# Hybrid decoder layer: the gate branch's convolutions issued in steps, another order of two products, and later column sums

## The chip, the cores and the metric

The kernel runs on one core of one Trainium2 chip. The metric is device time in microseconds (us) of one launch; the two kernels are compared by their runs on the same chip. Engines: PE (TensorE, matrix products), DVE (VectorE), ACT (ScalarE), POOL (GpSimd) and SP (SyncE, which issues the DMAs). PE reads its operands from SBUF and writes to PSUM banks, which DVE and ACT empty.

## What is computed

One layer of a decoder for 1024 prompt tokens and 32 sample tokens (1056 columns in all): a token mixer with three recurrences, then a gated feed-forward part with a causal convolution of width 3 on its gate branch. The change touches the feed-forward part and the norms just before it:

```python
def rms_norm(x, w):
    xf = x.astype(jnp.float32)
    y = xf * lax.rsqrt(jnp.mean(xf * xf, axis=-1, keepdims=True) + EPS)
    return (y * w.astype(jnp.float32)).astype(x.dtype)

def conv_ffn(h, ffn_state, w_up, conv_w, conv_b, w_down):
    up = jnp.einsum('bld,df->blf', h, w_up)              # w_up: 1024 x 5632
    gate, val = up[..., :D_FF], up[..., D_FF:]           # D_FF = 2816
    gate, new_state = causal_dwconv(gate, ffn_state, conv_w, conv_b)
    out = jnp.einsum('blf,fd->bld', jax.nn.gelu(gate, approximate=True) * val, w_down)
    return out, new_state.astype(ffn_state.dtype)

# in run_trunk
x = x + rms_norm(mix, norm_mix_post[l])
hn = rms_norm(x, norm_ffn_pre[l])
f, nf = conv_ffn(hn, ffn_s[l], ...)
x = x + rms_norm(f, norm_ffn_post[l])
```

## The kernel before

Everything is kept with the features on the 128 partitions and the 1056 tokens as columns, in four quarters of 264 columns. Every float32 product is done as three products of rounded halves (high x high, high x low, low x high), so a weight tile is first split: a cast on ACT (`wh`) and a subtraction on POOL or DVE (`wl`, L272 or L1834).

**Who orders the work.** The kernel's Python text makes several streams (generators), and `Weave` (L121 and after) takes turns among them by rank and by a planner's clock, `weave.now`, that counts matmul columns at 2.4 GHz: 0.11 us for one matmul of 264 columns, and four times that for one in plain float32. A stream that yields a number of nanoseconds, such as `WAIT["f_rows"]`, is continued once the planner's clock has gone that far. The instructions so issued go to a scheduler, which orders each engine's queue by priority (the order of issue, or 400 instructions earlier under `tc.high_priority(offset=AHEAD)`) among those whose inputs its own model of time holds for ready. On the chip each engine then runs its queue strictly in that order.

**The norms, `finish(q)` (L1603 and after).** For each quarter q the output projection's 8 row blocks (`product`, 24 matmuls each) are squared and summed into `sqs[q]`. `finish(q)` loads a quarter of x (one buffer, `x`, for all quarters), sums over the partitions by a matmul with ones (`rstd_of`, PSUM tile `po`), scales and adds (L1616, L1617), squares again on ACT into `sx`, adds on DVE into `ss` (L1624), waits `WAIT["f_rows"]`, sums over the partitions once more (the second `po`, which reads `ss`) and makes the operands of the next stage (L1634, L1581). `finish(1)` starts when `finish(0)` has made its x.

**The up projection.** From row block 4 on, pairs of row blocks are done as a `fast` task: a scheme of seven products of half-size blocks in place of eight, numbered p = 1 to 7, each for two halves u = 0, 1 of the columns. One product `run(p, u)` is 12 matmuls of 264 columns. Gate tasks (gate rows i) and value tasks (value rows i-1) alternate; i goes from 2 to 10, with a value task at either end, 20 tasks in all. Products 1, 6, 5, 2, 7 belong to the current task, while 4 and 3 of the task before are done between them, so that the list in `up()` (L1938) is the order of PE's queue:

`(1,0) (1,1) (6,0) (4,0)' (4,1)' (6,1) (3,0)' (3,1)' (5,0) (5,1) (2,0) (2,1) (7,0) (7,1)`

with a prime for the previous task's. In each u, 1 and 2 share a bank of `accp` (2 buffers), 6, 7 and 4 one of `accr` (5 buffers), 5 and 3 another. The bank of product 2 is emptied by a value task at L1817 (`hid`), and product 1 of the next task wants that buffer; (6,1) wants the bank that (4,0)' leaves, which a value task empties at L1810 (`rs`). With a gate task's product (3,1)' its `end()` is called: it issues both row blocks' `gate_conv` (L1772): small copies on POOL, a scaling on ACT (L217, Identity), two scalar_tensor_tensor instructions of 1072 columns on DVE (L1782), and Gelu on ACT. Its result `fy` is read by the value task after the next gate task.

**The weight pieces.** A product's weights are cast (L1833) and split (L1834) once for both u. `weight_piece` takes half tiles from a ring: two pieces share a pair of tiles (`wh`, `wl`), there are two such pairs, and a pair can be written again when every product that reads either half is done. The order of the pieces is 1, 6, 4', 3', 5, 2, 7. Since seven is odd, the pairs of a value task are (1, 6), (4', 3'), (5, 2), (7 and the next task's 1), and those of a gate task (6, 4'), (3', 5), (2, 7). So in a value task the piece of 5 can be cast once (6,1) is through. Products 2 and 4 split on DVE, the others on POOL. The sums that make the pieces (L1867 to L1872) run ahead of their task.

Of the kernel before, what the change touches and what calls it, by code (L numbers as in the profile page):

```python
# [8 lines left out]
F32 = mybir.dt.float32  # L9
# [7 lines left out]
P = 128  # L17
# [51 lines left out]
WAIT = dict(  # L69
    inv4=3140, blocks_in=7470, blocks_out=12000, inv=1760, out=3400, rows=3000, exp=690, gdn_unit=3720,  # L70
    norms=2680, kk=3700, scan1=460, scan2=1130, scan3=480, norm=6000, ml_unit=1120, ml_decay=1780, ml_kq=1330,
    ml_kw=1020, ml_scan=1070, ml_post=3000, gate=5000, ssd_x=1540, ssd_b=1170, ssd_decay=4000, ssd_scan=1020,
    ssd_unit=6650, ssd_post=2800, s_decay=3970, state=430, s_hop=2530, outer=760, s_ml=3230, s_out=2100,
    s_norm=6310, rows1=9000, rows2=6960, rows3=8500, f_rows=12500, f_wait=7000, f_piece=2600,
)

WARM = 8
# [77 lines left out]
def drain(gen):  # L155

    while True:
        try:
            next(gen)
        except StopIteration as e:  # L160
            return e.value
# [28 lines left out]
def bc(ap, ax, n):  # L190
    a = ap.unsqueeze(ax)
    s = list(a.shape)
    s[ax] = n
    return a.to_broadcast(s)
# [3 lines left out]
def kernel(ctx: ExitStack, tc: tile.TileContext, I, O):  # L198
# [17 lines left out]
    def act(**kw):  # L216
        i = nc.scalar.activation(**kw)  # L217
        if kw["func"] in (AF.Exp, AF.Tanh, AF.Gelu_apprx_tanh):
            others.append(i)
        return i  # L220
# [31 lines left out]
    def col(v, p=P, p0=0):  # L252
        return vec[p0:p0 + p, v:v + 1]
# [56 lines left out]
    def rstd_of(r, ssum):  # L310

        ps = sump.tile([P, 512], F32, name="po")
        n = r.shape[-1]
        for s in ssum:
            mm(ps[:, :n], lhsT=ones, rhs=s, start=(s is ssum[0]), stop=(s is ssum[-1]))
        log = nc.scalar.activation(out=r, in_=ps[:, :n], func=AF.Ln, scale=1.0 / D, bias=epsc)
        in_order(log, tables[-1])
        nc.scalar.activation(out=r, in_=r, func=AF.Exp, scale=-0.5)
        return r
# [51 lines left out]
    with ExitStack() as ph:  # L371
# [563 lines left out]
        pre, early_gdn = {}, {}  # L935
# [639 lines left out]
        def split_quarter(q, i, by_tile=False):  # L1575

            hi, lo = ops[q][0][i], ops[q][1][i]
            for a, b in [(k, k + 1) for k in range(KH)] if by_tile else [(0, KH)]:
                x = mx[:, KH * i + a:KH * i + b, quarters[q]]
                nc.scalar.copy(out=hi[:, a:b], in_=x)  # L1580
                vtt(out=lo[:, a:b], in0=x, in1=hi[:, a:b].bitcast(F32), op=ALU.subtract)  # L1581

        def new_operand(q):
            t = [block(hnp.tile([P, T], F32R, name=f"h{(0, 4, 13, 8)[q] + i}")) for i in range(4)]
            ops[q] = t[:2], t[2:]
# [17 lines left out]
        def finish(q):  # L1603
            if q:
                yield lambda: ("x", q - 1) in have
            x = on.tile([P, KD, Q], F32, name="x")
            dma(out=x, in_=I["xQ"][q])
            yield WAIT["f_wait"]
            s = sqs[q]
            r = rstd_of(on.tile([P, Q], F32, name="rstd", bufs=2), [s[:, 0, :], s[:, 1, :]])  # L1610
            sx = on.tile([P, KH, Q], F32, name="sx")
            s = on.tile([P, 2, Q], F32, name="ss", bufs=4)
            for i in range(2):
                ks = slice(KH * i, KH * i + KH)
                m = mx[:, ks, quarters[q]]
                vtt(out=m, in0=m, in1=bc(r, 1, KH), op=ALU.mult)  # L1616
                vtt(out=x[:, ks], in0=x[:, ks], in1=m, op=ALU.add)  # L1617
                if i == 0:
                    act(out=sx, in_=x[:, ks], func=AF.Square)
                    vtt(out=sx[:, 0:2], in0=sx[:, 0:2], in1=sx[:, 2:4], op=ALU.add)  # L1620
                else:
                    for a in (KH, KH + 2):
                        act(out=sx[:, 2:4], in_=x[:, a:a + 2], func=AF.Square)
                        vtt(out=sx[:, 0:2] if a == KH else s, in0=sx[:, 0:2], in1=sx[:, 2:4], op=ALU.add)  # L1624
                dma(out=x1_dram[q, :, ks], in_=x[:, ks])
            for k in range(KD):
                act(out=mix[k][:, quarters[q]], in_=x[:, k, :], func=AF.Copy, scale=col(V_FPRE + k))
            have.add(("x", q))
            yield WAIT["f_rows"]
            r = rstd_of(on.tile([P, Q], F32, name="rstd", bufs=2), [s[:, 0, :], s[:, 1, :]])  # L1630
            new_operand(q)
            for i in range(2):
                m = mx[:, KH * i:KH * i + KH, quarters[q]]
                vtt(out=m, in0=m, in1=bc(r, 1, KH), op=ALU.mult)  # L1634
                split_quarter(q, i)
            have.add(("normed", q))
# [56 lines left out]
    with ExitStack() as ph:  # L1693
# [4 lines left out]
        fo = []  # L1698
# [47 lines left out]
        def samp6(t, a):  # L1746
            return t[:, a:a + 48].rearrange("p (b s) -> p b s", s=6)
# [21 lines left out]

        ffn_io = {}  # L1770

        def gate_conv(f, pre):  # L1772
            st_ffn, ffn_o = ffn_io["st"], ffn_io["out"]
            y = fo[0].tile([P, 1074], F32, name="fy", bufs=4)
            blk = samp6(pre, 1026)
            nc.gpsimd.memset(pre[:, 0:2], 0.0)
            gcopy(out=blk[:, :, 0:2], in_=st_ffn[:, f, :].rearrange("p (b s) -> p b s", s=2))
            gcopy(out=ffn_o[:, f, 0:2], in_=pre[:, 1024:1026])
            gcopy(out=ffn_o[:, f, 2:18].rearrange("p (b s) -> p b s", s=2), in_=blk[:, :, 4:6])
            act(out=y[:, :LF], in_=pre[:, 2:2 + LF], func=AF.Identity, bias=col(V_FB + f), scale=col(V_FW + 3 * f + 2))  # L1780
            for j in (1, 0):
                stt(out=y[:, :LF], in0=pre[:, j:j + LF], scalar=col(V_FW + 3 * f + j), in1=y[:, :LF],  # L1782
                    op0=ALU.mult, op1=ALU.add)
            act(out=y[:, :LF], in_=y[:, :LF], func=AF.Gelu_apprx_tanh)
            return y

        def new_pre():
            return fg.tile([P, 1080], F32, name="fpre", bufs=4)
# [1 line left out]
        def gate_task(i):  # L1790
            pres = [new_pre() for j in range(2)]

            def out(j, h, u, x, ps):
                gate_in(pres[j], 2 * u + h, x, ps)

            def end():
                ys[i] = [gate_conv(2 * i + j, pres[j]) for j in range(2)]
            return fast(i, 0, out, end)

        def value_task(i):  # L1800
# [111 lines left out]
        ys = {}  # L1912

        def up():
            yield lambda: "projected" in have
            pres = [new_pre() for f in range(PLAIN)]
            for q in range(NQ):
                yield lambda: ("normed", q) in have
                for f in range(PLAIN):
                    ps = yield from dense(accr, held["up", f], operand, KD, q, Q)  # L1920
                    gate_in(pres[f], q, None, ps)
                have.add(("plain", q))
            yield lambda: "pieces" in have
            places.update({1: new_n(8, F32), 6: new_n(9, F32), "raw": new_n(10, F32)})
            ffn_io["st"] = fo[0].tile([P, NF, 16], F32, name="st_ffn")
            ffn_io["out"] = fo[0].tile([P, NF, 18], F32, name="ffn_o")
            dma(out=ffn_io["st"], in_=I["st_ffn"])
            tasks = [(value_task, 0)]
            for i in range(PLAIN // 2, NF // 2):
                tasks += [(gate_task, i), (value_task, i - 1)]  # L1930
            tasks.append((value_task, NF // 2 - 1))
            prev = None
            for n, (task, i) in enumerate(tasks):
                cur = task(i)
                if n == 0:
                    for i in range(PLAIN // 2):
                        ys[i] = [gate_conv(2 * i + j, pres[2 * i + j]) for j in range(2)]
                for p, u in ((1, 0), (1, 1), (6, 0), (4, 0), (4, 1), (6, 1), (3, 0), (3, 1),  # L1938
                             (5, 0), (5, 1), (2, 0), (2, 1), (7, 0), (7, 1)):
                    if p in (4, 3):  # L1940
                        if prev:
                            yield from prev.run(p, u)
                            if (p, u) == (3, 1):
                                prev.end()
                    else:
                        yield from cur.run(p, u)
                prev = cur
            for p, u in ((4, 0), (4, 1), (3, 0), (3, 1)):
                yield from prev.run(p, u)
            prev.end()  # L1950
            dma(out=O["ffn"], in_=ffn_io["out"])
# [5 lines left out]
        fo = fo[0]  # L1957
# [196 lines left out]
```

## Time and profile before

| | us |
|---|---|
| median of the 3 runs shown | 1596.19 (1593.82 to 1618.47) |
| the profiled execution, its own time | 1594.29 |
| span of its profile | 1592.5 |
| mean granted TensorE clock | 0.973 of full |

Stages in the profile: the mixer until about 720 us, the end of the mixer and the output projection with its norms until about 812, four plain gate row blocks until about 860, the 20 `fast` tasks until about 1310, the down projection to the end. Times in the profile are from the start of the span. PE's row counts matmuls whose ends are modelled; the idle time in front of an instruction is in square brackets, with what released it.

### The profile page before, as it was taken

What the parts mean: (1) busy time and instruction counts of PE and PEld (TensorE: products, weight loads), DVE (VectorE), ACT (ScalarE), POOL (GpSimd) and SP (SyncE); (2) the same over time, 40 slices, a digit from 0 to 9 for tenths busy, and PEclk for the clock granted to TensorE, in tenths of its full rate; (3) what the DMA queues carried; (4) which work ended last, traced back from release to release, by engine and by line L of the source; (5) the groups of instructions that cost most, each with busy time, mean ns of one, the idle gap of its engine ahead of it and who ended that gap; (6) DMA issues with size and microseconds to landing.
All of it is one profiled execution on the core that took longest, in us unless ns stands there. A gap on an engine that the chain in (4) does not pass through costs nothing.

```text
span 1592.5 us, 27521 instructions
## 1 busy us (share of the span) xinstructions
PE 1461.3 (92%) x10756; PEld 1414.0 (89%) x10756; DVE 1014.6 (64%) x2019; ACT 622.1 (39%) x1348; POOL 587.2 (37%) x666
## 2 busy tenths in 40 slices
PE   9788998989999989896899999999999999999995
PEld 8788898979989989894899988889999899999995
DVE  6898878795484366626578566666565666234457
ACT  7653544433432332434566223333332234111244
POOL 6244333232444542564224323333333232212323
PEclk9999999999999999998899999999999999999998
DMA  6011111011121232224330212221212126312303
GB/s 218 29 49 29 32 37 34 25 30 30 56 61 40 69 112 83 81 93 148 135 121 32 81 68 81 74 73 42 81 68 81 68 94 232 126 45 96 118 28 137
DMA packets 59786, 124.92 MB, mean 78 GB/s; under 512 B 15480, under 2 KB 21496, under 8 KB 58632
## 3 DMA queue, kind: packets, MB, share of 16 engines
q1 hardware_dynamic: 59656, 123.16, 23.2%
q8 instruction: 85, 1.39, 0.4%
q14 instruction: 45, 0.37, 0.1%
HBM read 97.40 MB, written 25.21 MB: 77 GB/s over the span
## 4 chain that ended last, share of the span: by engine, by line
PE 52%; DVE 25%; ACT 8%; issue 6%; POOL 5%; DMA 3%; SPq 0%; DVEq 0%; ACTq 0%; POOLq 0%
PE acc L208 43%; DVE fy L1782 4%; PE mb L208 3%; PE mc L208 3%; DVE kq L471 2%; DMA E<-rows_dram 2%; PE mb L212 2%; POOL wl L1834 2%; ACT wh L1833 1%; PE po L208 1%; DVE ws L1867 1%; DVE two L790 1%; DVE v L471 1%; POOL E L874 1%; ACT fy L217 1%
## 5 line engine op out<-in xcount | busy, mean ns | idle before, releaser
L208 PE MATMUL acc<-h,wh 128*128 128x264 f32 (+1 forms) x3040 | 680.5, 314 | 38.9 <-DVE hid L1817 21.7
L208 PEld LDWEIGHTS acc<-h,wh 128*128 128x128 f32 x3040 | 498.8, 192 | 48.6 <-ACT fy L217 23.4
L208 PE MATMUL acc<-h,wl 128*128 128x264 f32 (+1 forms) x1528 | 467.4, 306 | 2.6 <-POOL wl L272 2.4
L208 PEld LDWEIGHTS acc<-h,wl 128*128 128x128 f32 x1528 | 291.8, 191 | 3.9 <-POOL wl L272 2.6
L208 PE MATMUL acc<-hidl,wh 128*128 128x264 f32 x576 | 163.7, 284 | 0.5 <-DVE hidl L1973 0.5
L208 PE MATMUL acc<-hidh,wh 128*128 128x264 f32 x576 | 163.9, 285 | 0.0
L208 PE MATMUL acc<-hidh,wl 128*128 128x264 f32 x576 | 163.5, 284 | 0.0
L1834 POOL TENSOR_TENSOR wl<-ws,wh 128x512 fp32r<-128x512 f32 x60 | 82.6, 1384 | 179.1 <-ACT wh L1833 179.1
L1996 DVE TENSOR_TENSOR fa<-fa,acc 128x264 f32<-128x264 f32 x160 | 68.0, 427 | 124.7 <-PE acc L208 123.9
L272 POOL TENSOR_TENSOR wl<-w,wh 128x1024 fp32r<-128x1024 f32 x42 | 102.9, 2451 | 51.6 <-ACT wh L271 48.1
L208 PE MATMUL acc<-n,wh 128*128 128x264 f32 x640 | 119.0, 284 | 1.2 <-DVE n L1902 1.2
L208 PEld LDWEIGHTS acc<-hidl,wh 128*128 128x128 f32 x576 | 108.6, 189 | 0.8 <-DVE hidl L1973 0.8
L1834 POOL TENSOR_TENSOR wl<-w,wh 128x512 fp32r<-128x512 f32 x40 | 62.9, 1574 | 124.4 <-ACT wh L1833 118.6
L208 PEld LDWEIGHTS acc<-hidh,wl 128*128 128x128 f32 x576 | 108.6, 189 | 0.0
L208 PEld LDWEIGHTS acc<-hidh,wh 128*128 128x128 f32 x576 | 108.5, 188 | 0.0
L1987 POOL TENSOR_TENSOR wl<-w,wh 128x1024 fp32r<-128x1024 f32 (+1 forms) x22 | 47.6, 2164 | 148.2 <-ACT wh L1986 145.2
L208 PE MATMUL acc<-r,wh 128*128 128x264 f32 x480 | 90.8, 286 | 11.7 <-DVE rs L1810 11.7
L208 PEld LDWEIGHTS acc<-n,wh 128*128 128x128 f32 x640 | 99.1, 189 | 1.4 <-issue 1.4
L208 PE MATMUL acc<-n,wl 128*128 128x264 f32 x320 | 90.8, 284 | 0.0
L208 PEld LDWEIGHTS acc<-r,wh 128*128 128x128 f32 x480 | 74.2, 188 | 13.5 <-DVE rs L1810 13.5
L1782 DVE SCALAR_TENSOR_TENSOR fy<-fpre,vec,fy 128x1072 f32<-128x1072 f32 x44 | 75.8, 1775 | 13.4 <-ACT fy L217 13.3
L1986 ACT CAST wh<-w 128x1024 fp32r<-128x1024 f32 (+1 forms) x22 | 20.5, 933 | 132.2 <-PE acc L208 127.5
(527 smaller groups left out, 3042.3 us busy)
## 6 DMA issues: line engine op xcount, KB each, us to landing
w<-in_w_in_dram SPq DMA_DIRECT2D x30, 512.0 KB
w<-in_w_up_dram SPq DMA_DIRECT2D x60, 256.0 KB
hid_dram<-hid SPq DMA_DIRECT2D x22, 528.0 KB
hidl<-hid_dram SPq DMA_DIRECT2D x21, 528.0 KB
w<-in_w_dn_dram SPq DMA_DIRECT2D x17, 512.0 KB
w<-in_w_out_dram SPq DMA_DIRECT2D x16, 512.0 KB
E<-rows_dram SPq DMA_DIRECT2D x24, 256.0 KB
n<-in_w_up_dram SPq DMA_DIRECT2D x20, 256.0 KB
```

The costliest lines, as they stand in the source:

```text
L208: return nc.tensor.matmul(out, **kw)
L212: return nc.tensor.transpose(out, in_, identity)
L217: i = nc.scalar.activation(**kw)
L272: tt(out=wl[:, ks], in0=w[:, ks], in1=wh[:, ks].bitcast(F32), op=ALU.subtract)
L471: stt(out=y[:, a:b], in0=pre[:, a + j:b + j], scalar=cw2[:, 4 * t + j:4 * t + j + 1], in1=y[:, a:b], op0=ALU.mult, op1=ALU.add)
L790: vtt(out=two[pr], in0=NT[pr, :, pr], in1=bc(con[pr, C_LOW:C_LOW + 2 * B16], 1, 4), op=ALU.mult)
L874: gtt(out=E, in0=E, in1=bc(con[:, mask:mask + P], 1, n), op=ALU.add)
L1782: stt(out=y[:, :LF], in0=pre[:, j:j + LF], scalar=col(V_FW + 3 * f + j), in1=y[:, :LF], op0=ALU.mult, op1=ALU.add)
L1834: tt(out=wl, in0=x, in1=wh.bitcast(F32), op=ALU.subtract)
L1986: nc.scalar.copy(out=wh, in_=w)
L1987: gtt(out=wl, in0=w, in1=wh.bitcast(F32), op=ALU.subtract)
L1996: vtt(out=fa[:, q, m, :], in0=fa[:, q, m, :], in1=ps[:, :Q], op=ALU.add)
```

## The change

Three edits. `gate_conv` becomes a generator with four steps (copies and Identity, each of the two scalar_tensor_tensor, Gelu), its result tile being made by `end()` through `new_y`. `end()` puts the two generators on a list, and `up()` takes one step of it after every product with u = 1, seven times a task. In the list of products (3,0)' and (6,1) change places. `WAIT["f_rows"]`, 12.5 us for every quarter, becomes 24, 15.5, 15.5 and 12.5 us. The number of instructions stays as it is.

```diff
--- before.py
+++ after.py
@@ -71,7 +71,7 @@
     norms=2680, kk=3700, scan1=460, scan2=1130, scan3=480, norm=6000, ml_unit=1120, ml_decay=1780, ml_kq=1330,
     ml_kw=1020, ml_scan=1070, ml_post=3000, gate=5000, ssd_x=1540, ssd_b=1170, ssd_decay=4000, ssd_scan=1020,
     ssd_unit=6650, ssd_post=2800, s_decay=3970, state=430, s_hop=2530, outer=760, s_ml=3230, s_out=2100,
-    s_norm=6310, rows1=9000, rows2=6960, rows3=8500, f_rows=12500, f_wait=7000, f_piece=2600,
+    s_norm=6310, rows1=9000, rows2=6960, rows3=8500, f_rows=(24000, 15500, 15500, 12500), f_wait=7000, f_piece=2600,
 )
 
 WARM = 8
@@ -1626,7 +1626,7 @@
             for k in range(KD):
                 act(out=mix[k][:, quarters[q]], in_=x[:, k, :], func=AF.Copy, scale=col(V_FPRE + k))
             have.add(("x", q))
-            yield WAIT["f_rows"]
+            yield WAIT["f_rows"][q]
             r = rstd_of(on.tile([P, Q], F32, name="rstd", bufs=2), [s[:, 0, :], s[:, 1, :]])
             new_operand(q)
             for i in range(2):
@@ -1769,20 +1769,35 @@
 
         ffn_io = {}
 
-        def gate_conv(f, pre):
+        def new_y():
+            return fo[0].tile([P, 1074], F32, name="fy", bufs=4)
+
+        def gate_conv(f, pre, y):
+
             st_ffn, ffn_o = ffn_io["st"], ffn_io["out"]
-            y = fo[0].tile([P, 1074], F32, name="fy", bufs=4)
             blk = samp6(pre, 1026)
             nc.gpsimd.memset(pre[:, 0:2], 0.0)
             gcopy(out=blk[:, :, 0:2], in_=st_ffn[:, f, :].rearrange("p (b s) -> p b s", s=2))
             gcopy(out=ffn_o[:, f, 0:2], in_=pre[:, 1024:1026])
             gcopy(out=ffn_o[:, f, 2:18].rearrange("p (b s) -> p b s", s=2), in_=blk[:, :, 4:6])
             act(out=y[:, :LF], in_=pre[:, 2:2 + LF], func=AF.Identity, bias=col(V_FB + f), scale=col(V_FW + 3 * f + 2))
+            yield
             for j in (1, 0):
                 stt(out=y[:, :LF], in0=pre[:, j:j + LF], scalar=col(V_FW + 3 * f + j), in1=y[:, :LF],
                     op0=ALU.mult, op1=ALU.add)
+                yield
             act(out=y[:, :LF], in_=y[:, :LF], func=AF.Gelu_apprx_tanh)
-            return y
+            yield
+
+
+        later = []
+
+        def one_later():
+            while later:
+                if next(later[0], 0) == 0:
+                    later.pop(0)
+                else:
+                    break
 
         def new_pre():
             return fg.tile([P, 1080], F32, name="fpre", bufs=4)
@@ -1794,7 +1809,8 @@
                 gate_in(pres[j], 2 * u + h, x, ps)
 
             def end():
-                ys[i] = [gate_conv(2 * i + j, pres[j]) for j in range(2)]
+                ys[i] = [new_y() for j in range(2)]
+                later.extend(gate_conv(2 * i + j, pres[j], ys[i][j]) for j in range(2))
             return fast(i, 0, out, end)
 
         def value_task(i):
@@ -1934,8 +1950,10 @@
                 cur = task(i)
                 if n == 0:
                     for i in range(PLAIN // 2):
-                        ys[i] = [gate_conv(2 * i + j, pres[2 * i + j]) for j in range(2)]
-                for p, u in ((1, 0), (1, 1), (6, 0), (4, 0), (4, 1), (6, 1), (3, 0), (3, 1),
+                        ys[i] = [new_y() for j in range(2)]
+                        for j in range(2):
+                            drain(gate_conv(2 * i + j, pres[2 * i + j], ys[i][j]))
+                for p, u in ((1, 0), (1, 1), (6, 0), (4, 0), (4, 1), (3, 0), (6, 1), (3, 1),
                              (5, 0), (5, 1), (2, 0), (2, 1), (7, 0), (7, 1)):
                     if p in (4, 3):
                         if prev:
@@ -1944,6 +1962,8 @@
                                 prev.end()
                     else:
                         yield from cur.run(p, u)
+                    if u:
+                        one_later()
                 prev = cur
             for p, u in ((4, 0), (4, 1), (3, 0), (3, 1)):
                 yield from prev.run(p, u)
```

## Rows read from the trace of the kernel before

**Rows 1.** The page's first two lines: the span and PE's share.
```profile
span 1592.5 us, 27521 instructions
PE 1461.3 (92%) x10756; PEld 1414.0 (89%) x10756; DVE 1014.6 (64%) x2019; ACT 622.1 (39%) x1348; POOL 587.2 (37%) x666
```

**Rows 2.** What PE waited for, whole span: total us, times, longest.
```profile
PE acc L208 <- DVE hid L1817: 21.7, 9, 2.4
PE po L208 <- DVE ss L1624: 17.1, 3, 12.2
PE acc L208 <- DVE rs L1810: 11.7, 9, 1.4
```

**Rows 3.** Chain of waits, 780 to 1310 us: start, us, what.
```profile
966.93 4.41 PE acc L208 x23
...
1013.31 3.06 PE acc L208 x23
...
1022.15 21.98 PE acc L208 x179
...
1284.66 22.16 PE acc L208 x168
```

**Rows 4.** Timeline around a value task's end, DVE and PE: start, us, instruction [idle before].
```profile
1004.47 7.15 DVE L1782 SCALAR_TENSOR_TENSOR fy<-fpre,vec,fy 128x1072 f32<-128x1072 f32 x4 [1.39 <-ACT fy L217]
...
1012.75 0.76 DVE L1817 TENSOR_TENSOR hid<-fy,acc 128x264 f32<-128x264 f32 x2
...
1013.31 0.48 PE L208 MATMUL acc<-h,wh 128*128 128x264 f32 x2 [2.41 <-DVE hid L1817]
```

**Rows 5.** Timeline early in a gate task, DVE and PE.
```profile
1018.46 1.75 DVE L1867 TENSOR_TENSOR ws<-w 128x512 f32<-128x512 f32 x1 [2.85 <-POOL wl L1834]
...
1021.08 0.68 DVE L1870 TENSOR_TENSOR w<-w 128x512 f32<-128x512 f32 x1
1021.68 0.41 DVE L1810 TENSOR_TENSOR rs<-n,acc 128x264 f32<-128x264 f32 x1
...
1022.15 0.51 PE L208 MATMUL acc<-r,wh 128*128 128x264 f32 x2 [1.32 <-DVE rs L1810]
```

**Rows 6.** Timeline in a value task, ACT, POOL, PE: the piece of 5.
```profile
999.06 0.41 PE L208 MATMUL acc<-h,wh 128*128 128x264 f32 x2
...
999.19 0.62 ACT L1833 CAST wh<-ws 128x512 fp32r<-128x512 f32 x1 [5.35 <-PE acc L208]
...
999.89 1.29 POOL L1834 TENSOR_TENSOR wl<-ws,wh 128x512 fp32r<-128x512 f32 x1 [6.58 <-ACT wh L1833]
...
1001.99 0.41 PE L208 MATMUL acc<-n,wh 128*128 128x264 f32 x2
```

**Rows 7.** Timeline, POOL and DVE: a piece beside L1782, L1782 alone, an early memset.
```profile
1004.58 2.37 POOL L1834 TENSOR_TENSOR wl<-w,wh 128x512 fp32r<-128x512 f32 x1
...
865.74 1.33 DVE L1782 SCALAR_TENSOR_TENSOR fy<-fpre,vec,fy 128x1072 f32<-128x1072 f32 x1
...
987.83 0.11 POOL L1776 MEMSET fpre<- 128x2 f32 x1
```

**Rows 8.** Timeline of the norms, PE, SP, ACT and DVE.
```profile
739.78 1.96 PE L208 MATMUL po<-ss,ones 128*128 128x264 f32 x4
...
759.55 2.13 PE L208 MATMUL po<-ss,ones 128*128 128x264 f32 x4 [12.17 <-DVE ss L1624]
...
810.56 1.16 PE L208 MATMUL po<-ss,ones 128*128 128x264 f32 x4 [1.65 <-DVE ss L1624]
...
757.17 1.72 ACT L217 ACTIVATE mix<-x,vec 128x264 f32<-128x264 f32 x4
...
759.34 0.37 SPq L1607 DMA_DIRECT2D x<-in_xQ_dram  x1
...
767.44 2.42 DVE L1617 TENSOR_TENSOR x<-x,mix 128x1056 f32<-128x1056 f32 x2
...
772.92 0.71 DVE L1624 TENSOR_TENSOR ss<-sx 128x528 f32<-128x528 f32 x1 [0.71 <-ACT sx L217]
```

## Prediction, as put on record before the run

> **What bounds the kernel now.** I read the page's shares first: PE is busy 92% of the span [rows 1], so whatever does not let PE run on earlier is worth nothing, and the most that can be won is PE's idle time and the time at a lower clock. PE's waits over the whole span came next [rows 2]: three of the groups there belong to the three edits, 21.7 us for `hid` (9 times), 11.7 us for `rs` (9 times) and 17.1 us for the second column sum (3 times), 50.5 us together. The reader is to see that the first two are small waits that come back once in each pair of tasks, and the third is mostly one wait of 12.17 us. Then the chain of waits over the `fast` tasks [rows 3], for what a matmul costs and what a wait does to the clock: 179 matmuls take 21.98 us, 0.1228 us each, so a product of 12 takes 1.47 us. The 23 matmuls behind a wait for `hid` take 3.06 us in one pair and 4.41 us in another. Last the timelines around one wait of each kind.
>
> **The wait for `hid`.** At 1004.47 DVE starts the four L1782 of a gate task's `end()` in one block, 7.15 us [rows 4]. Product (2,0) of the value task has begun meanwhile and is through at about 1006.4, but L1817, which empties its bank, stands behind the block and two weight sums and starts at 1012.75. PE has done (2,1) and (7,0), (7,1) by 1010.9 and stands for 2.41 us until (1,0) of the next task gets the bank. The change issues the four L1782 one to every second product, so that at most one is issued between two emptyings of banks. Three products lie between the end of (2,0) and (1,0), 3 x 1.47 = 4.4 us. One L1782 costs 1.33 us alone [rows 7] and 7.15 / 4 = 1.79 us in the block; even a block of two (3.6 us) ahead of L1817 (0.4 us) would be through in time. I take the wait as gone: -21.7 us, bounds 0 and -21.7. Where the stall goes: (4,0) wants the reads of (7,0), which have 1.47 us for each of the four products (7,1), (1,0), (1,1), (6,0), so nothing is late next there.
>
> **The clock.** The longer runs of matmuls stand behind waits for `hid`: 4.41 - 3.06 = 1.35 us, twice in the nine pairs, and at 1284.66 168 matmuls take 22.16 us where 168 x 0.1228 = 20.6, 1.5 us more [rows 3]. Without the 2.4 us waits in front I take these as gone too: -4.2 us, bounds 0 and -4.2.
>
> **The wait for `rs`.** In a gate task PE wants the bank that (4,0)' leaves for (6,1). L1810, which empties it, stands behind the sums made ahead for the next task, L1867 (1.75 us, begun only when POOL has freed its tile), L1868 and L1870 (0.68 each), and ends at 1021.68 + 0.41 = 1022.09; PE waits 1.32 us [rows 5]. (3,0)' now runs in that gap: it needs no new bank, and its piece, whose split is what L1867 waits for, is ready at 1018.46, while PE falls idle at 1022.15 - 1.32 = 1020.83. PE would want the bank 1.47 us later, at 1022.3. So -11.7 us, with a margin of only 0.1 to 0.2 us; bound on the other side below, with the rivals.
>
> **What the new order costs.** In a value task the piece of 5 can be cast once (6,1) is through. There (6,1) ended at 999.06, the cast began at 999.19 and POOL was done at 999.89 + 1.29 = 1001.18, 2.1 us behind (6,1); (5,0) began at 1001.99 behind two products, and nothing waited [rows 6]. With (3,0)' ahead of (6,1), one product is left between, 1.47 us, and the third matmul of (5,0), the first that reads `wl`, comes 0.25 us later. 2.1 - 1.72 = 0.4 us, in the 10 value tasks that have a task in front: +4.0 us. PE's whole queue stands behind that matmul; the banks have time to spare then. The lower bound is 0; the upper one stands with the rivals. The other pairs keep 2.3 us or more: that of 3' and 5 in a gate task has (6,0), (4,0)', (4,1)', 4.4 us, for the same 2.1, and that of 2 falls from 5.9 to 4.4 us.
>
> **The steps themselves** are the same instructions on the same engines. The Identity and the Gelu on ACT and the copies on POOL move by at most half a task, and their reader is more than a task away. I cost them at nothing; their cover is that ACT and POOL are busy 39% and 37% [rows 1]. No DMA is moved past another by any of the three edits.
>
> **The later sums.** `finish(1)` starts its first sum at 739.78 [rows 8]. It stands 7 us (`f_wait`) behind the place from which `finish(0)`'s `f_rows` counts. From there the planner now gives 15.5 us to `finish(1)`'s second sum and 24 - 7 = 17 us to `finish(0)`'s, in place of 12.5 and 5.5: the two change places. By the planner's 0.11 us a matmul, less 0.88 for the first sum itself, `finish(1)`'s second sum now stands behind 133 matmuls, where it stood behind 108. 42 of them are done when PE falls idle at 759.55 - 12.17 = 747.4, the other 91 take 11.2 us, so PE gets there at about 758.6. But its input is the L1624 that ended at 772.92 + 0.71 = 773.6, and this does not hang on PE: x has one buffer, which ACT left at 757.17 + 1.72 = 758.9, its load was issued at 759.34, and L1617 ran at 767.44. So the wait of 12.17 us goes from one sum to the other. What is won is the order on DVE: L1634 and L1581 of `finish(0)` no longer run ahead of L1617, which can start when the load lands. I estimate 1 to 2 us from that, and 31 matmuls more done by the second sum against a longer stretch at half clock come out within 1 us. I take -1.5 us; bounds +3 (three emptyings of banks, on ACT ahead of the copy that frees x) and -18 (both waits gone and PE not slowed). For quarter 2 the wait of 1.65 us [rows 8] has 3 us more: -1.7. Sum of this edit: -3.2.
>
> **Sum.** -21.7 - 4.2 - 11.7 + 4.0 - 3.2 = -36.8 us, on the profiled execution's own 1594.3 us (its span is 1592.5, 1.8 lie around it, and it is 1.9 us under the median of the runs shown): 1557.5, say 1558 us, 2.3% less. 2% is about what a measurement of this kernel can tell from no change; it lies at 1562.
>
> **Rivals.**
> - *The scheduler puts the steps back together.* The order of issue is not the order of a queue: POOL ran the memset of L1776 at 987.83, 14 us before the place where `end()` issues it [rows 7]. If DVE again gets four L1782 in a row, the waits for `hid` and the clock stay and 11.7 - 4.0 + 3.2 = 10.9 us are won: 1583. Against it: an emptying of a bank is now issued ahead of three of the four, so that the scheduler must prefer it once ready. Chance 0.12.
> - *`rs` still waits.* If one L1782 of the second row block, now issued in the gate task, starts ahead of L1810, the margin of 0.1 is gone and PE waits 1.2 to 1.7 us in 9 gate tasks: about 13 us, 1571. For it: DVE idles 2.85 us ahead of L1867, where such a step fits only if it starts early [rows 5]. Chance 0.15.
> - *A step meets the piece that PE waits for.* A POOL split takes 1.29 us alone [rows 6] and 2.37 beside L1782 [rows 7]. If a step ran beside the piece of 5, the new wait would be 0.4 + 1.1 = 1.5 us in 10 tasks: 11 us more, 1569. For it: four steps are spread over two tasks now; against it, by issue the steps end with (3,1) of the gate task, before any value task's (6,1). Chance 0.10. By the Trainium skill's page "SBUF — State Buffer", section "Who interferes with whom", a VectorE instruction with two SBUF inputs contends with a GpSimd instruction that reads SBUF, and spreading such instructions speaks against this change; here the trace agrees, with 1.29 and 2.37 us.
> - *Slower: Gelu blocks the casts.* ACT runs in order. If Gelu is queued ahead of a pair's cast, the cast waits for the second L1782, which may now come two gaps of 2.95 us behind the first, up to 5.9 us. The pairs have up to 2.3 us to spare. Above 1.8 us lost per task, 20 tasks eat up the 37 us and the kernel is slower than before; at 5.9 - 2.3 = 3.6 us it is 72 us, 1630. Against it: each Gelu is issued last. Chance 0.07.
> - *Both long waits for the sums go.* If x is free earlier or PE finds more products, up to 18 us in place of 1.5: 1541. Chance 0.06.
>
> **How the numbers follow.** The forecast has 0.50 and a range of its own of 1549 to 1566 (the clock's 4.2 not won, or the piece of 5 not waiting and 3 us more of the sums). Below 1562 lie 0.42 of it, the last rival and the milder half of the two at 1570 in part: faster 0.50. The two at 1570, the first and the rest of the forecast: same 0.45. Slower by over 2% takes nearly the whole of the fourth: 0.05. The range reaches over the cases up to 1584 and to part of the last: 1545 to 1584.
>
> **What would show it.** Right: no wait for `hid` or `rs` among PE's, a wait of about 0.4 us for POOL's `wl` ten times, a pair of tasks in 336 x 0.1228 + 0.4 = 41.7 us where that from 966.93 to 1013.31 takes 46.4 (45.0 without the clock's share), one L1782 at a time between L1817s, and PE's wait ahead of `finish(1)`'s second sum above 10 us. Wrong: L1782 four in a row; L1810 behind L1782; casts behind Gelu; pairs above 43 us.

## The result, and the profile after

| | before | after |
|---|---|---|
| median, us | 1598.26 (18 runs, 1591.95 to 1618.47) | 1596.07 (18 runs, 1569.17 to 1599.86) |
| ratio of the undisturbed runs | 1 | 0.987, 95% interval 0.983 to 0.991 |
| profiled execution, span, us | 1592.5 | 1595.3 |

The changed kernel is 1.3% faster, between 0.9% and 1.7%: less than the 2% that counts as a difference here. One thing is needed to read its median: in the profiled execution TensorE ran at half clock from 658 to 706 us, where both kernels issue the same matmuls in the same order, 10 of the 18 runs lie as high (near 1597) with as low a mean clock (0.955 to 0.960), and the ratio leaves them out. The profile below is therefore read stage by stage; the stretch itself is taken up with the seventh to the ninth experiment.

The page of after begins so, as [rows 1]:

```profile
span 1595.3 us, 27520 instructions
PE 1480.2 (93%) x10756; PEld 1430.2 (90%) x10756; DVE 1014.4 (64%) x2019; ACT 621.1 (39%) x1348; POOL 581.2 (36%) x666
```

What PE of after waited for from 600 us on (total us, times, longest), to be put beside [rows 2]:

```profile
PE po L208 <- DVE ss L1624: 15.4, 1, 15.4
PE acc L208 <- DVE rs L1826: 13.3, 9, 1.7
...
PE acc L208 <- POOL wl L1850: 3.6, 11, 0.6
...
PE po L208 <- POOL ss L1601: 2.5, 1, 2.5
PE acc L208 <- POOL wl L272: 2.4, 1, 2.4
```

`hid` is gone from the list: 21.7 us are won. `rs` (L1826 is L1810 of before) is not: 13.3 us where it was 11.7. The new wait for the piece of 5 (L1850 is L1834) is there with 3.6 us. The waits for the sums are 15.4 + 2.5 where they were 17.1.

The chain of waits of after through one pair of tasks (start, us, what), beside [rows 3]:

```profile
909.49 21.98 PE acc L208 x179
932.24 1.30 POOL wl L1850
933.58 13.14 PE acc L208 x106
947.68 1.31 POOL wl L1850
949.01 1.77 DVE ws L1883
952.71 21.98 PE acc L208 x179
```

A pair takes 952.71 - 909.49 = 43.22 us, where it was 45.0 or 46.4. The eight pairs between the waits for `rs` of after are alike (43.2 us), and none has the longer run of matmuls that stood behind three of the nine waits for `hid` before. Matmuls take 336 x 0.1228 = 41.26 us of it, the piece of 5 0.31, `rs` 1.65. The chain also names who is late: POOL's `wl`, then DVE's L1883, which is L1867 of before.

The timeline of DVE at the end of the value task in that pair of after (start, us, instruction, [idle before]), beside [rows 4]:

```profile
937.53 2.58 DVE L1786 SCALAR_TENSOR_TENSOR fy<-fpre,vec,fy 128x1072 f32<-128x1072 f32 x2 [1.35 <-ACT fy L217]
940.03 0.42 DVE L1833 TENSOR_TENSOR hid<-fy,acc 128x264 f32<-128x264 f32 x1
940.37 2.19 DVE L1786 SCALAR_TENSOR_TENSOR fy<-fpre,vec,fy 128x1072 f32<-128x1072 f32 x1
942.49 0.41 DVE L1833 TENSOR_TENSOR hid<-fy,acc 128x264 f32<-128x264 f32 x1
...
944.37 1.32 DVE L1786 SCALAR_TENSOR_TENSOR fy<-fpre,vec,fy 128x1072 f32<-128x1072 f32 x1
```

The four steps still run within one value task: the scheduler draws them together into 8.2 us. But L1833, the emptying that stood behind all four, now stands between them, at 940.03 and 942.49, and PE takes the bank without a wait.

ACT, POOL, DVE and PE of after where `rs` is late, beside [rows 5]:

```profile
945.72 1.10 ACT L217 ACTIVATE fy<-fy 128x1072 f32<-128x1072 f32 x1 [2.02 <-DVE fy L1786]
...
946.29 0.42 DVE L1833 TENSOR_TENSOR hid<-fy,rs 128x264 f32<-128x264 f32 x1
...
946.73 0.36 ACT L1915 COPY n<-acc 128x264 f32<-128x264 f32 x1
946.98 1.14 ACT L1849 CAST wh<-ws 128x512 fp32r<-128x512 f32 x2
...
947.68 2.54 POOL L1850 TENSOR_TENSOR wl<-ws,wh 128x512 fp32r<-128x512 f32 x2 [6.25 <-ACT wh L1849]
...
949.01 1.76 DVE L1883 TENSOR_TENSOR ws<-w 128x512 f32<-128x512 f32 x1 [1.43 <-POOL wl L1850]
...
952.24 0.42 DVE L1826 TENSOR_TENSOR rs<-n,acc 128x264 f32<-128x264 f32 x1
...
952.71 0.51 PE L208 MATMUL acc<-r,wh 128*128 128x264 f32 x2 [1.65 <-DVE rs L1826]
```

The piece of 3' could be cast when (1,1) is through, and the matmuls behind (1,1) begin at 945.10. But ACT stands idle for 2.02 us at the head of its queue with the second row block's Gelu, which waits for the fourth L1786, and runs it at 945.72; the casts follow at 946.98. POOL and L1883 are late by as much, L1883 takes 1.76 us beside POOL's second split, and L1826 ends 1.65 us after PE has wanted the bank.

The piece of 5, as [rows 6]: PE of after loses 0.31 us, and POOL's split in front takes 1.29 us, so no step runs beside it.

```profile
932.24 1.29 POOL L1850 TENSOR_TENSOR wl<-ws,wh 128x512 fp32r<-128x512 f32 x1 [8.04 <-ACT wh L1849]
...
933.58 0.39 PE L208 MATMUL acc<-n,wl 128*128 128x264 f32 x1 [0.31 <-POOL wl L1850]
```

The norms of after on PE, SP, DVE and ACT, beside [rows 8]:

```profile
762.16 1.05 PE L208 MATMUL po<-ss,ones 128*128 128x264 f32 x4
...
797.19 2.13 PE L208 MATMUL po<-ss,ones 128*128 128x264 f32 x4 [15.40 <-DVE ss L1624]
...
843.36 1.16 PE L208 MATMUL po<-ss,ones 128*128 128x264 f32 x4 [2.46 <-POOL ss L1601]
...
784.08 0.33 SPq L1607 DMA_DIRECT2D x<-in_xQ_dram  x1
...
791.19 2.43 DVE L1617 TENSOR_TENSOR x<-x,mix 128x1056 f32<-128x1056 f32 x2 [8.72 <-DMA x<-in_xQ_dram]
...
776.61 1.05 ACT L271 CAST n<-w 128x1024 fp32r<-128x1024 f32 x1 [3.01 <-DMA w<-in_w_out_dram]
777.56 0.64 ACT L217 ACTIVATE sx<-x 128x528 f32<-128x528 f32 x1
```

The same squaring on ACT in before, where it stands ahead of that cast:

```profile
753.73 0.64 ACT L217 ACTIVATE sx<-x 128x528 f32<-128x528 f32 x1 [2.80 <-DVE x L1617]
```

The two waits of 12.17 and 3.24 us have become one of 15.40. Counted from `finish(1)`'s first sum, the load of x is issued at 784.08 - 762.16 = 21.9 us, where it was 759.34 - 739.78 = 19.6. The wait of 1.65 us for quarter 2 is gone, and 2.46 us for quarter 3's first sum have come.

### The profile page after: what moved, and what is told of

Read it like the earlier page. It is cut to its first block, busy times and chain, and to the rows that moved or that the text cites. A ratio compares the mean times of both kernels' runs of the same rounds, so it can differ in the third digit from the quotient of the medians.

```text
span 1595.3 us, 27520 instructions
## 1 busy us (share of the span) xinstructions
PE 1480.2 (93%) x10756; PEld 1430.2 (90%) x10756; DVE 1014.4 (64%) x2019; ACT 621.1 (39%) x1348; POOL 581.2 (36%) x666
## 5 line engine op out<-in xcount | busy, mean ns | idle before, releaser
L208 PE MATMUL acc<-h,wh 128*128 128x264 f32 (+1 forms) x3040 | 687.1, 317 | 15.8 <-DVE pre L308 11.7
L208 PEld LDWEIGHTS acc<-h,wh 128*128 128x128 f32 x3040 | 505.4, 195 | 23.3 <-DVE pre L308 8.0
L208 PEld LDWEIGHTS acc<-h,wl 128*128 128x128 f32 x1528 | 295.5, 193 | 3.9 <-POOL wl L272 2.6
L1850 POOL TENSOR_TENSOR wl<-ws,wh 128x512 fp32r<-128x512 f32 x60 | 77.6, 1301 | 191.2 <-ACT wh L1849 191.2
L272 POOL TENSOR_TENSOR wl<-w,wh 128x1024 fp32r<-128x1024 f32 x42 | 104.7, 2493 | 54.3 <-ACT wh L271 50.8
L208 PE MATMUL acc<-r,wh 128*128 128x264 f32 x480 | 91.0, 287 | 13.3 <-DVE rs L1826 13.3
L1850 POOL TENSOR_TENSOR wl<-w,wh 128x512 fp32r<-128x512 f32 x40 | 59.2, 1488 | 81.8 <-ACT wh L1849 81.8
L208 PEld LDWEIGHTS acc<-r,wh 128*128 128x128 f32 x480 | 74.3, 188 | 15.4 <-DVE rs L1826 15.2
L1786 DVE SCALAR_TENSOR_TENSOR fy<-fpre,vec,fy 128x1072 f32<-128x1072 f32 x44 | 67.3, 1548 | 14.9 <-ACT fy L217 14.8
```

Source lines behind the costliest of these rows:

```text
L208: return nc.tensor.matmul(out, **kw)
L272: tt(out=wl[:, ks], in0=w[:, ks], in1=wh[:, ks].bitcast(F32), op=ALU.subtract)
L1850: tt(out=wl, in0=x, in1=wh.bitcast(F32), op=ALU.subtract)
```

## Experiments

**One edit at a time.** Three kernels, each the one before with one edit of the change.

```diff
-            yield WAIT["f_rows"]
+            yield WAIT["f_rows"][q]           # 24000, 15500, 15500, 12500
```


> The kernel before with the later sums alone. Theory: the wait of 12.17 us only moves to the other sum and the gain is given back. One wait of about 15 us for ss ahead of a column sum where before shows 12.17, 3.24 and 1.65 us, a new wait of about 2.5 us ahead of quarter 3's first sum, and from that sum's predecessor to the first gate task no more than 2 us either way. The rival, as forecast: 3 us are won between those two places. The tasks keep 21.7 us of waits for hid and 11.7 for rs, 45.0 us a pair.

Measured (e1), in one run: 1615.47 us, with a granted clock of 0.61 from 660 to 680 us, ahead of the norms that the edit is about. The waits are 16.0 us for the moved sum and 2.5 us for quarter 3's, and from `finish(0)`'s first sum to the first chain piece of the gate tasks it takes 158.3 us where the kernel before takes 154.8. By this one pair of profiles the edit loses 3.5 us where the forecast had a gain of 3.2.

```diff
-                for p, u in (... (4, 0), (4, 1), (6, 1), (3, 0), (3, 1),
+                for p, u in (... (4, 0), (4, 1), (3, 0), (6, 1), (3, 1),
```


> The kernel before with the order of products 3 and 6 alone. Theory: without steps Gelu does not stand ahead of the casts when PE gets there (PE has waited for hid), so the wait for rs falls from 1.3 to 0.1 or 0.2 us a pair, the wait for the piece of 5 comes in at 0.35 us, that for hid stays at 2.4: a pair in 41.3 + 2.4 + 0.5 = 44.2 us for 45.0. Rival, that the sums made ahead on DVE hold L1810 back by themselves: rs keeps above 1 us, a pair takes 45 us or more.

Measured (e2), in one run: 1598.76 us. PE's largest group of waits over the whole span:

```profile
PE acc L208 <- DVE hid L1817: 27.2, 9, 3.0
```

The windows around one of these waits (stretch, its length, busy us of PE, PEld, DVE, ACT and POOL with their instructions, granted clock, DMA share, GB/s):

```profile
1010.00:1013.00 3.00, 0.38 (x2) 0.41 (x3) 3.00 (x6) 1.10 (x1) 0.00 (x0) 0.87 0.11 22
1013.00:1016.00 3.00, 3.00 (x16) 3.00 (x16) 1.93 (x7) 0.36 (x1) 0.00 (x0) 0.56 0.43 158
1016.00:1019.00 3.00, 3.00 (x27) 3.00 (x26) 0.00 (x0) 1.44 (x4) 1.18 (x1) 1.00 0.00 0
```

`rs` is gone from the list, as forecast for the new order, and the piece of 5 costs 0.31 us in a pair. But `hid` waits 3.0 us in place of 2.4, and behind that the clock falls to 0.56 of full in each pair, where before it did in three of nine: the pair takes 46.1 us, 1.9 more than was expected. By itself the new order wins nothing.

The third has the steps (`new_y`, `gate_conv` as a generator, `one_later`) with the old order and the old sums.

> The kernel before with the steps alone, products and sums in the order of before. Theory, Gelu ahead of the casts: no wait for hid, none for the piece of 5, but a wait for rs of 1.65 + 1.47 = 3.1 us a pair, longer than before's 1.3: a pair in 44.4 us. Rival, that the swap of the products causes what is left of the wait for rs: rs at 1.3 us as before, a pair in 42.6 us.

Measured (e3), in one run: 1592.55 us; no wait for `hid`; `rs` 16.4 us, 1.88 in a pair, and behind seven of these eight waits the windows of 5 us have a granted clock of 0.66. Such a pair takes 44.40 us as expected, but with 1.2 us less of the wait and about as much lost to the clock; the one pair without the loss takes 42.9. The steps are what removes `hid`. A pair takes 45.4 us on average in before, 46.1 with the order alone, 44.4 with the steps alone and 43.2 with both: the order pays only beside the steps.

**Gelu and the casts.** In the changed kernel each Gelu is put behind the cast that was issued last before it (`in_order` is an order for the scheduler alone). The first row block's Gelu keeps its place by this, the second's now stands behind the cast of the piece of 3':

```diff
-            act(out=y[:, :LF], in_=y[:, :LF], func=AF.Gelu_apprx_tanh)
+            gelu = act(out=y[:, :LF], in_=y[:, :LF], func=AF.Gelu_apprx_tanh)
+            if casts:
+                in_order(gelu, casts[-1])
 ...
-            nc.scalar.copy(out=wh, in_=x)
+            casts.append(nc.scalar.copy(out=wh, in_=x))
```


> The changed kernel with one more rule for the scheduler: the second row block's Gelu stands behind the cast of the piece of 3 on ACT. Nothing else is moved. Theory: the cast starts 1.8 us earlier, L1810 with it; the wait for rs falls from 1.65 to about 0.16 us a pair, what the first gate task of the changed kernel shows, which has no Gelu in the way; pairs in 41.7 us for 43.2, 12 to 13 us less in all, about 1562 us. Rival, that the sums ahead on DVE or POOL's split hold L1810 back: rs stays above 1 us, pairs at 43 us, the time unchanged.

Measured (e4): 1565.0 and 1565.9 us in the two executions without the half-clock stretch. The ratio to the kernel before is 0.982 (0.975 to 0.990), but two of the four runs in it have the stretch; e7 against e9 below, both without it, puts the edit at 1573.16 - 1562.76 = 10.4 us. Waits of PE:

```profile
PE acc L208 <- DVE rs L1828: 4.2, 9, 0.5
PE acc L208 <- POOL wl L1853: 3.0, 10, 0.3
```

The timeline of ACT, DVE and PE in a gate task:

```profile
987.49 1.14 ACT L1852 CAST wh<-ws 128x512 fp32r<-128x512 f32 x2 [1.01 <-PE acc L208]
...
988.80 1.10 ACT L217 ACTIVATE fy<-fy 128x1072 f32<-128x1072 f32 x1
...
988.56 1.21 DVE L1835 TENSOR_TENSOR hid<-fy,rs 128x264 f32<-128x264 f32 x1
...
991.21 0.68 DVE L1886 TENSOR_TENSOR ws<-w 128x512 f32<-128x512 f32 x1
...
993.83 0.51 PE L208 MATMUL acc<-r,wh 128*128 128x264 f32 x2 [0.50 <-DVE rs L1828]
```

The casts now wait for PE alone, and `rs` falls from 13.3 to 4.2 us. The pair takes 42.05 us, 1.17 less, where 1.5 was expected. In the way is now DVE's L1835 with both inputs in SBUF (`fy`, `rs`): it takes 1.21 us beside POOL's split, where the same one took 0.42 us in after with no split beside it (946.29), and L1886 stands behind it. This is the contention that the Trainium skill's page "SBUF — State Buffer", section "Who interferes with whom", tells of; the trace agrees, with 1.21 against 0.42 us. The `hid` that reads a PSUM bank takes 0.42 us at 940.03 of after, though a split starts beside it at 940.13. How much of the missing 0.3 us is this was not tested.

**The sums, set otherwise.** The kernel of e4 with another order of the second sums, and with the old one:

```diff
-  f_rows=(24000, 15500, 15500, 12500)
+  f_rows=(26000, 31000, 22000, 12500)     # e5
+  f_rows=(12500, 12500, 12500, 12500)     # e6
```


> The kernel of e4 with f_rows = (26000, 31000, 22000, 12500): finish(0)'s second sum comes first and finish(1)'s is set back behind the end of its L1624, so that PE has the plain products to do in place of the wait of 15.1 us for DVE ss L1624. Theory (the wait is only an order: the input of finish(1)'s second sum is ready 35 us behind po(1#1) whatever PE does, and PE reaches it 15 us too early): the wait is 0 to 3 us, no other wait of PE grows by more than 3 us, and the kernel takes 12 to 15 us less than e4. Rival (the operands are the bound: the plain products of quarter 1 and the first gate task need what this sum releases, by way of ACT and DVE): the wait of 15 us comes back ahead of those products under the name of h or n operands, and the time is within 3 us of e4.

Measured (e5): 1557.8 to 1560.0 us in the three executions without the half-clock stretch, 6 us under e4's; 12 to 15 were expected. e4 ran on another chip, but the profiles agree: from `finish(0)`'s first sum to quarter 3's second it takes 843.23 - 743.84 = 99.4 us in place of 105.5. The wait of 15.1 us is gone, and in its place stand others, the two longest of which are:

```profile
PE acc L208 <- ACT ss L217: 6.6, 1, 6.6
...
PE po L208 <- ACT rstd L316: 4.2, 1, 4.2
```

> The kernel of e4 with the sums set as in the kernel before (12500 for all four). Theory (the later sums cost 1 to 3.5 us here, as e1 showed): waits for the second sums 12.2 and 3.2 us as in the kernel before, the stretch from finish(0)'s first sum to quarter 3's second one about 104 us against 105.5 in e4, the pairs of tasks 42.05 us as in e4, and the kernel 1 to 3.5 us faster than e4. The forecast's own term: e4 is the faster by 3.2 us.

Measured (e6): 1560.6, 1561.9 and 1566.4 us without the stretch, in the middle 3.5 us under e4's. The wait for the first of the sums is 13.3 us, one of 3.2 follows. Of the 3.5 us the norms show 1.2: from `finish(0)`'s first sum to quarter 3's second 104.3 us, where e4 takes 105.5, both as expected. So the later sums cost 1 to 3.5 us; no pair of kernels has them win.

**The stretch at half clock.** One line is moved, so that the second `w_out` weight is cast and split ahead of quarter 2's operand:

```diff
                 for q in range(2):
                     yield from product(m, w, q)
-                if m == 0:
+                if m == 1:
                     split_mix(2)
```


> The kernel of e4 with split_mix(2) of project_first issued behind the products of m = 1 in place of m = 0, so that the cast and the split of the second w_out weight run ahead of the casts of quarter 2's operand. It takes away the 2.37 us that PE waits for POOL wl L272 at 654.4 us of the changed kernel, ahead of the stretch at half clock; the matmuls that follow are the same in the same order. Theory (the half clock of 657 to 705 us hangs on that wait): the wait is below 0.5 us, the granted clock stays 1.00 there, and the stretch from 657 to 705 us takes some 24 us less than in the profile of the changed kernel. Rival (the kind of the matmuls that follow brings the half clock, not the wait): the wait is gone and the granted clock still falls to 0.50 there for 15 us or more in a part of the executions. Besides, 2 us are won by the wait itself.

> The kernel before with split_mix(2) of project_first issued behind the products of m = 1, as in e7, and nothing of the change. Theory (what the wait of 2.37 us for POOL wl L272 sets off is the same in every kernel, and the kernel before meets it in a part of its executions, those of 1607 to 1618 us): the wait is gone, the granted clock is 1.00 from 660 to 720 us, the executions lie at 1589 to 1600 us and none above 1603; waits for hid 21.7 and rs 11.7 us as in the kernel before. Rival (the long executions of the kernel before come from elsewhere): executions above 1607 us stay.

> The changed kernel with the same one line moved, and nothing of e4. Theory (the change itself is worth 20 us: hid 21.7 and its clock 4.1 won, rs waits 1.6 us more, the piece of 5 waits 3.6 us, the later sums cost about 1 to 2.5): executions at 1567 to 1576 us, none above 1582, median 1571; against e8, median to median, 20 to 25 us less, about 1.4%; rs waits 13.3 us and the pairs take 43.2 us as in the changed kernel. Rival (the stretch at half clock belongs to the change): executions near 1596 us stay. The forecast's own sum would put it at 1555.

| | median, us | lowest to highest | runs |
|---|---|---|---|
| e7: e4 with the line moved | 1562.76 | 1560.79 to 1565.91 | 6 |
| e8: before with the line moved | 1594.45 | 1589.93 to 1599.80 | 12 |
| e9: after with the line moved | 1573.16 | 1569.03 to 1575.31 | 6 |

The windows of after and then of e9 over that stretch (columns as above):

```profile
640.00:660.00 20.00, 16.52 (x114) 15.65 (x112) 18.06 (x37) 14.02 (x30) 8.95 (x9) 0.95 0.29 100
660.00:680.00 20.00, 20.00 (x92) 19.05 (x92) 1.31 (x4) 2.90 (x7) 8.97 (x7) 0.50 0.11 36
680.00:700.00 20.00, 20.00 (x94) 17.34 (x93) 2.12 (x7) 3.35 (x8) 6.96 (x9) 0.50 0.12 43
700.00:720.00 20.00, 20.00 (x127) 16.43 (x127) 4.44 (x11) 4.25 (x13) 8.41 (x7) 0.86 0.14 55
```
```profile
640.00:660.00 20.00, 19.32 (x151) 18.61 (x150) 19.27 (x37) 13.83 (x30) 11.71 (x11) 1.00 0.26 84
660.00:680.00 20.00, 20.00 (x154) 16.40 (x153) 3.10 (x10) 5.86 (x15) 13.86 (x15) 1.00 0.25 79
680.00:700.00 20.00, 20.00 (x158) 18.74 (x159) 5.14 (x11) 6.71 (x18) 12.86 (x10) 1.00 0.22 80
700.00:720.00 20.00, 18.73 (x148) 17.88 (x147) 6.44 (x12) 6.97 (x18) 15.39 (x10) 1.00 0.32 106
```

With the line moved the wait for `wl` L272 is 0.4 us in place of 2.4, the clock stays full, and in 20 us PE starts 154 matmuls where it started 92. The stretch costs 20.9 us: from the end of that wait to `finish(0)`'s first sum, over the same matmuls, it takes 96.4 us in after and 75.5 in e9, and in none of the 24 executions of the three kernels does the time show such a loss. The kernel before was profiled without the stretch, but its longest executions (1617.6 us at a mean clock of 0.957) are gone with the line moved too: e8 has none above 1599.8. So the stretch does not seem to belong to the change; how often it comes may still hang on it, since 10 of 18 executions of after lie so high and 5 of 18 of before above 1608. Without it, e9 against e8 gives the change's own worth: 1594.45 - 1573.16 = 21.3 us, 1.3%, as the ratio above. The wait is not the whole cause. Eight kernels were profiled with a wait of 2.4 us there: behind it the clock is 1.00 in before, e2 and e6 (75.5 us to the first sum), at 0.50 for 17 us in e1, e3 and e5 (83.4) and for 48 us in after and e4 (96.4). What decides between them was not found. The line moves other instructions on ACT, POOL and DVE besides.

**All together.** e7 with the sums of e5.

> e7 with the sums of e5: f_rows = (26000, 31000, 22000, 12500). Theory (the two gains are in different stages and add up: e5's executions without the stretch at half clock, 1558 to 1560 us, lie 5 to 7 us under those of e4, 1565): median 1555 to 1559 us, against 1562.8 of e7; waits of 6.6 us for ACT ss L217 and 4.2 us for ACT rstd L316 in place of 15 us for DVE ss L1624. Rival (what is won there is given back behind it): within 2 us of e7.

Measured (e10): 1557.92 us median (1555.99 to 1561.78, 6 runs), ratio to the kernel before 0.974, interval 0.971 to 0.977. This is the fastest of all, 15 us under e9. In the stage of the norms PE waits 8.7 us for `ss` L217, 4.3 for `rstd` and 1.8 for `sq`, 14.8 together, where e7 waits 16.2 + 2.5 + 0.6 = 19.3; the medians differ by 4.8. So the gain adds to e7's, but three quarters of the wait have only moved, now to the banks that ACT empties (`ss`, `sq`).

## Why the forecast came out as it did

The forecast was 1557.5 us, -36.8; the change is worth 21.3, which on the same base is 1594.3 - 21.3 = 1573.0 us. That lies within 1545 to 1584, a range that reaches so far for the rivals' sake, and outside the forecast's own 1549 to 1566. That it falls beside the 1571 of the rival "`rs` still waits" is in part luck: the cause that this rival named did not occur. Term by term, from the two profiles:

| term | forecast | measured |
|---|---|---|
| `hid` | -21.7 | -21.7 |
| clock behind it | -4.2 | -4.1 |
| `rs` | -11.7 | +1.6 |
| piece of 5 | +4.0 | +3.6 |
| later sums | -3.2 | about +1 |
| sum | -36.8 | -19.6 |

- *`hid` and the clock*: right, with the mechanism (an emptying between the steps), though not by spreading the steps. The first rival, that the scheduler puts the steps back together, is half true: they are together again, and the emptyings go between them, which was the reason given against it.
- *`rs`*: this step failed. It took the piece of 3' to be ready as early as in the kernel before: L1867 began 1022.3 - 1018.46 = 3.8 us ahead of PE's want there, and L1883 begins 951.06 - 949.01 = 2.1 us ahead of it now. The swap of (3,0)' and (6,1) gives PE its 1.47 us, as e2 shows without the steps (no wait for `rs`). But the steps bring a Gelu ahead of the cast of that piece. The rival "`rs` still waits" has the place and the price (about 13 us), with L1782 on DVE as the cause; the cause is the one of the rival "Gelu blocks the casts", which was priced at up to 3.6 us a task and held to a chance of 0.07 by the order of issue. It costs less than that and once in a pair, and e4 shows it: with that Gelu behind the cast 9.1 of the 13.3 us go. So the step that said that the steps cost nothing on ACT, because it is busy 39% only and their reader is far away, failed with it: what counted was who stands behind them in the queue.
- *The piece of 5*: right, 0.31 us for 0.4.
- *The later sums*: the change of places and a wait above 10 us came as worked out. The gain did not: what was taken as -1.5 from the order on DVE is eaten by the load of x, which is issued 2.3 us later. Emptyings of banks now stand on ACT ahead of the copy that frees x, which was the reason given for the bound of +3, but that is only a part. The rest the forecast did not have: ACT's queue now holds the cast of a `w_out` weight ahead of the first squaring of the second half of x and stands 3.01 us for the weight's load, so that the squaring begins 777.56 - 762.16 = 15.4 us behind `finish(1)`'s first sum, where it began 753.73 - 739.78 = 13.95 behind it. All seven profiled kernels with later second sums have this order, the five with the old ones do not; it was not tested by itself. For quarter 2 the -1.7 came and was given back at quarter 3's first sum, 2.46 us, which the sum had left out. From `finish(1)`'s first sum to the same matmul of the first gate task it takes 909.49 - 762.16 = 147.3 us, where it took 885.75 + 1.47 - 739.78 = 147.4 (in after one product more lies ahead of that place). But before lost 1.35 us to a wait for `rs` on the way and after 0.16, so the edit costs about 1 us there, and 1 to 3.5 in the other pairs of kernels.
- *A step meets the piece*: it did not; the split takes 1.29 us.
- *What shows it*: pairs of 43.2 us, above the 43 named as wrong, and casts behind Gelu, which was named too. Of the signs of being right, "one L1782 at a time" failed: two run ahead of the first emptying, at 937.53, and `hid` went all the same.

The remaining 21.3 - 19.6 = 1.7 us are within the spread of single executions (e8 alone spans 9.9).

## What to carry to other kernels

A piece of work cut into steps is worth most for what may now run between the steps; before counting a second gain on the same path, follow each instruction of the moved steps through the in-order queue of its engine, here the Gelu on ACT, and ask what it waits for and who stands behind it; the share of time that the engine is free does not tell. Moving a wait for an operand gains nothing until the operand itself comes earlier or there is other work to put in its place. A stretch at half clock can cost as much as a change is worth, here 20.9 against 21.3 us: look at the granted clock by windows before comparing two kernels.

## What the runs showed of the hardware

TensorE's granted clock can stay at its lower level, 0.50 of full (1.2 GHz), while PE is busy all the time: in after from 658 to 706 us, with 48.00 of 48.00 us busy (the ends of matmuls are modelled), and the stage of these matmuls takes 96.4 us in place of 75.5. By the Trainium skill's page "TensorE: Matmul & The Clock Gate", section "Part 1: The HAM clock gate (the "warmup" mystery)", activity releases the throttle; for 48 us here it did not. PE had waited 2.4 us for `wl` just before, and the same wait left the clock at 1.00 in the profiled executions of before, e2 and e6. In the pairs of tasks the clock fell behind all nine waits of 3.0 us (e2), behind seven of eight of 1.9 us (e3), behind three of nine of 2.4 us (before; four of nine in e1 and in e8) and behind none of eight of 1.65 us (after). So the length of the wait alone does not decide.
